# Hybrid decoder layer on one core: v of branch B summed feature block by feature block, all gates of A and B as block-product pairs

## Chip, cores, metric

One core of a Trainium2 chip runs the kernel. The metric is the device time of one execution in microseconds, lower is better. All inputs and outputs lie in HBM and are fp32.

## What is computed

One layer over 1024 prompt tokens and 8 sample tokens, width D = 1024, branches of width 512 (cut from the reference; RMSNorm, LayerNorm and the depthwise convolution are as usual):

```python
mod = jax.nn.silu(c) @ w_ada + b_ada
shift, scale, gate = jnp.split(mod[:, None, :], 3, axis=-1)
h = _rmsnorm(x, norm_g) * (1 + scale) + shift
p = h @ w_in
a_b, a_c, a_h, a_g, b_u, b_v, b_g, c_x, c_g, m_a, m_b, m_c = jnp.split(p, IN_SPLITS, axis=-1)
conv_out, conv_new = _short_conv(a_c * a_h, conv_prev, conv_w, conv_b)
y_a = a_b * conv_out * jax.nn.silu(a_g)
u = jax.nn.gelu(b_u)
v = _layernorm(jax.nn.gelu(b_v), lnv_g, lnv_b)
y_b = _spatial_gate(u, v, sgu_w, sgu_b) * jax.nn.silu(b_g)
...
merged = (jax.nn.sigmoid(m_a) * (y_a @ w_branch[0])
          + jax.nn.sigmoid(m_b) * (y_b @ w_branch[1])
          + jax.nn.sigmoid(m_c) * (y_c @ w_branch[2]))
x = x + gate * (merged @ w_out)
```

`_spatial_gate` mixes v inside blocks of 128 tokens with one lower triangular 128 x 128 matrix per head, adds a bias and multiplies by u.

## The kernel before

**Layout.** Activations lie with the features on the partitions: a tile is 128 features x 1032 tokens. The 1032 columns are two halves of 516 (512 prompt tokens and 4 sample tokens each), so h is eight such tiles, `hhi` and `hlo`. Every fp32 product is three matmuls of rounded parts: high x high, high x low, low x high. A part is made by a copy on ScalarE (high) and a subtraction on VectorE (low), the helper at L86/87.

**Pairs.** Two output tiles of 128 features that share h can be had as one pair (`pair_jobs`, L504 to L567). The contraction is split into two halves of the features and the tokens into their two halves; seven block products of 24 matmuls of 258 columns take the place of eight. For that, sums and differences of token halves of h are needed (`t_sums` L465 to L476, `t_split`, and `t1_split`, which overwrites the first half of hhi and hlo), as are sums of weight blocks, made on VectorE ahead of each pair. A plain tile, not paired, takes 24 x 1032 columns.

**Front and k-loop.** The tokens are cut into three column chunks, `QC`: 416, 360 and 256. The first chunk of x is loaded, squared and summed; from its norm the scale is spread over the partitions (`row_sums` L205, `rsqrt_mean` L212 to L217, `spread` L226, `rstd_all` L241). A conditioning step for each of the eight feature blocks k (`ada_mm` L288, `ada_tr` L296 to L301) gives its scale and shift columns. Then the k-loop runs over the eight feature blocks: h of block k + 1 is built for the first chunk (`h_norm` L247, `h_mod` L254 to L264, `h_lo` L268) while TensorE adds the block k to six output tiles, the four of u and two of the gates of B (`mm3` L357 to L359). The squares of the other chunks are summed on ScalarE and GpSimd inside the loop (`add_square` L195 to L199), and h for them is built at its end; `g1_job` then computes the six tiles for chunks two and three.

**After it.** `bvs_mm` and eight `bv_job` (L697 to L699, 24 matmuls of 512 columns each) give v with tokens on the partitions. Between and behind them run the two other gates of B as plain tiles (`bg_job`), the LayerNorm of v, the sums of token halves (`t_jobs`), four mixing jobs (`sgu_job`, L790 to L805), which multiply u in place (`gate_u` L642), and two plain tiles of A (`ac0`, `ah0`). Then 23 pairs follow, the first of them `ag0`, then `az1`, `ag1` and so on; the merges of the three branches; and the output projection (L1155 to L1157).

**What sets the order.** Each engine runs its instructions in the order in which they are written. A list of `Job`s holds for each: its DMA, its split, its matmuls and its post-work; the planner issues the DMA and the split of a job the stated number of microseconds of matmul time ahead (`ahead`), and puts small post-work (`later`) behind that, as room comes. All loads go by one DMA queue (SP). Matmuls named `warm` (L317) compute nothing that is used; they stand in TensorE's queue among the first row sums.

Of the kernel before, what the change touches and what calls it, by code (L numbers as in the profile page):

```python
# [51 lines left out]
def hybrid_step_kernel(ctx: ExitStack, tc: tile.TileContext, ins, outs):  # L52
# [114 lines left out]
    def load_w1(k):  # L167
        t = S(f"w1r{k}", NG1 * P)
        Q.dma_start(t, ins["w1"][k])
        return t  # L170

    def sum_squares(xk):
        n, nb = QC[0][1:3]
        ps = PS("ss0")
        for k in range(KD):
            sq = S(f"sq0_{k}", n)
            if k == KD - 1:
                V.tensor_tensor(sq, xk[k], xk[k], ALU.mult)
            else:
                A_.activation(sq, xk[k], AF.Square)  # L180
            if k % 2:
                V.tensor_tensor(sq, sq, prev, ALU.add)
                row_sums(ps, sq, n, nb, k == 1, k == KD - 1)
                warm_up(2 if k < 5 else 0)
            prev = sq
        return ps

    def add_square(c, k, xk, acc):

        n = QC[c][1]  # L190
        if k == 0:
            acc[c] = S(f"sqa{c}", n)
        sq = sm.tile([P, 512], F32, tag="sq", name=f"sq{c}_{k}")[:, :n] if k else acc[c]
        if c == 1:
            A_.activation(sq, xk[k], AF.Square)  # L195
        else:
            G_.tensor_tensor(sq, xk[k], xk[k], ALU.mult)
        if k:
            G_.tensor_tensor(acc[c], acc[c], sq, ALU.add)  # L199
# [50 lines left out]
    def h_mod(c, k, th):  # L250
        c0, m, _, at_ = QC[c]
        t, h = th[:, :m], th[:, m:]
        if c == 0:
            V.tensor_scalar(h, t, Ac[:, k, 0:1], Sc[:, k, 0:1], ALU.mult, ALU.add)  # L254
        else:
            for a, b in ((0, at_), (at_ + HS, m)):
                if a < b:
                    A_.activation(h[:, a:b], t[:, a:b], AF.Identity, scale=Ac[:, k, 0:1], bias=Sc[:, k, 0:1])
            s = slice(at_, at_ + HS)
            j = HS * (c - 1)  # L260
            V.tensor_tensor(h[:, s], t[:, s], Ac[:, k, 1 + j : 1 + j + HS], ALU.mult)
            V.tensor_tensor(h[:, s], h[:, s], Sc[:, k, 1 + j : 1 + j + HS], ALU.add)
            V.tensor_copy(hs[:, k, j : j + HS], h[:, s])
        A_.activation(hhi[k][:, c0 : c0 + m], h, AF.Copy)  # L264

    def h_lo(c, k, th):
        c0, m = QC[c][:2]
        V.tensor_tensor(hlo[k][:, c0 : c0 + m], th[:, m:], f32(hhi[k][:, c0 : c0 + m]), ALU.subtract)  # L268

    def build_h(c, ks):  # L270

        th = {}
        n = len(ks)
        for i in range(n + 2):
            if i < n:
                th[i] = h_norm(c, ks[i])
            if 0 <= i - 1 < n:
                h_mod(c, ks[i - 1], th[i - 1])
            if i - 2 >= 0:
                h_lo(c, ks[i - 2], th[i - 2])  # L280
# [1117 lines left out]
```

## Time and profile before

| | |
|---|---|
| device time, median of 3 runs | 953.38 us (951.3 to 953.74) |
| the profiled execution | 952.71 us, of which its span 950.6 us |
| TensorE busy | 915.3 us, 96% |
| VectorE busy | 553.9 us, 58% |
| ScalarE busy | 350.2 us, 37% |
| GpSimd busy | 48.2 us, 5% |
| share of the chain that ended last | TensorE 86%, VectorE 8%, ScalarE 3% |

The span is the time between the first and the last recorded instruction; the rest of the device time lies outside it. A busy time is summed over the whole span, so it averages over stages with different limits. The chain that ended last is followed back from the last instruction: at each step to what released it or to the instruction before it on the same engine. The rows further below are read with these two in mind: a window shows which engine is full in a stretch, a wait shows who was late there, and the time line shows each instruction's start, its duration and, in brackets, the idle time before it with its releaser. A matmul's duration in a row includes the way through the array; the pace is read from the starts.

### The profile page before, as it was taken

The page shows a single profiled execution, that of the slowest core. Times are in us where ns is not written, and L with a number is a line of the kernel's source. Part 1 is how long each engine was busy: PE and PEld are TensorE (multiplying, and loading weights), DVE is VectorE, ACT ScalarE, POOL GpSimd, SP SyncE. Part 2 cuts the span into 40 slices and gives each one's busy share as a digit, 9 for nine tenths or more (in the row PEclk, how much of TensorE's full clock was granted, in tenths as well). Part 3 has the DMA queues.
Part 4 walks back from the last instruction along what each step waited for, and adds up shares of the span by engine and source line. Part 5 has one row for each costly group of instructions (what it writes and reads, how often), then busy time and mean ns, then how long its engine had stood idle before and what let it go on. Part 6 is the DMA issues. An engine that isn't in the chain of part 4 may idle for free.

```text
span 950.6 us, 16189 instructions
## 1 busy us (share of the span) xinstructions
PE 915.3 (96%) x6742; PEld 882.3 (93%) x6742; DVE 553.9 (58%) x1047; ACT 350.2 (37%) x638; POOL 48.2 (5%) x69
## 2 busy tenths in 40 slices
PE   9979999879999999999999999999999999999995
PEld 7759888779999999999999999999999799999995
DVE  4585324698666666665666657644452558673635
ACT  4449525422423334334534534443432310430210
POOL 1250202220000000000000000000000000000001
PEclk7999999989999999999999999999999999999998
DMA  9801400033211122142041330432379826161013
GB/s 336 332 1 46 152 4 23 13 111 131 70 46 68 46 70 85 38 156 90 20 182 45 137 110 1 168 124 100 146 301 376 311 68 222 45 195 30 30 38 112
DMA packets 45466, 108.82 MB, mean 114 GB/s; under 512 B 11465, under 2 KB 18377, under 8 KB 45393
## 3 DMA queue, kind: packets, MB, share of 16 engines
q1 hardware_dynamic: 45392, 107.79, 32.3%
q8 instruction: 53, 0.87, 0.4%
q14 instruction: 21, 0.16, 0.0%
HBM read 83.93 MB, written 23.84 MB: 113 GB/s over the span
## 4 chain that ended last, share of the span: by engine, by line
PE 86%; DVE 8%; ACT 3%; issue 1%; DMA 1%; POOL 0%; SPq 0%; DVEq 0%; ACTq 0%; POOLq 0%
PE o L1155 3%; PE o L1157 3%; PE o L1156 3%; PE g_0B L540 2%; PE g_2B L542 2%; PE g_3B L542 2%; PE g_0B L542 2%; PE g_2B L540 2%; PE g_3B L540 2%; PE g_2B L543 2%; PE g_1B L540 2%; PE g_1B L543 2%; PE g_1B L542 2%; PE g_3B L543 2%; PE g_0B L543 2%; PE bv L697 2%
## 5 line engine op out<-in xcount | busy, mean ns | idle before, releaser
L1155 PE MATMUL o<-mh,woh 128*128 128x388 f32 (+1 forms) x192 | 62.0, 323 | 0.0
L1157 PE MATMUL o<-mh,wol 128*128 128x388 f32 (+1 forms) x192 | 61.4, 320 | 0.0
L1156 PE MATMUL o<-ml,woh 128*128 128x388 f32 (+1 forms) x192 | 61.4, 320 | 0.0
L357 PE MATMUL g<-hhi,w1h 128*128 128x416 f32 (+2 forms) x144 | 48.0, 333 | 2.2 <-ACT hhi L264 2.2
L358 PE MATMUL g<-hlo,w1h 128*128 128x416 f32 (+2 forms) x144 | 46.9, 326 | 1.6 <-DVE hlo L268 1.1
L359 PE MATMUL g<-hhi,w1l 128*128 128x416 f32 (+2 forms) x144 | 46.1, 320 | 0.0
L1155 PEld LDWEIGHTS o<-mh,woh 128*128 128x128 f32 x192 | 36.1, 188 | 0.3
L1156 PEld LDWEIGHTS o<-ml,woh 128*128 128x128 f32 x192 | 36.1, 188 | 0.3
L1157 PEld LDWEIGHTS o<-mh,wol 128*128 128x128 f32 x192 | 36.1, 188 | 0.0
L357 PEld LDWEIGHTS g<-hhi,w1h 128*128 128x128 f32 x144 | 27.2, 189 | 5.1 <-ACT hhi L264 2.8
L358 PEld LDWEIGHTS g<-hlo,w1h 128*128 128x128 f32 x144 | 27.1, 188 | 4.2 <-DVE hlo L268 3.8
L1258 ACT ACTIVATE osq<-xr 128x388 f32<-128x388 f32 (+1 forms) x21 | 10.3, 491 | 48.4 <-DVE xr L1247 28.1
L359 PEld LDWEIGHTS g<-hhi,w1l 128*128 128x128 f32 x144 | 27.1, 188 | 0.1
L86 ACT ACTIVATE mh<-acc 128x516 fp32r<-128x516 f32 (+1 forms) x14 | 9.2, 688 | 44.0 <-DVE acc L1046 44.0
L697 PE MATMUL bv<-bvh,hhi 128*128 128x512 f32 x64 | 25.3, 396 | 0.0
L698 PE MATMUL bv<-bvl,hhi 128*128 128x512 f32 x64 | 25.3, 395 | 0.0
L699 PE MATMUL bv<-bvh,hlo 128*128 128x512 f32 x64 | 25.2, 394 | 0.0
L717 DVE BATCH_NORM_STATS2 bn<-v 128x6 f32<-128x512 f32 x8 | 5.6, 694 | 29.5 <-ACT v L715 29.5
L264 ACT ACTIVATE hhi<-th 128x416 fp32r<-128x416 f32 (+2 forms) x24 | 11.8, 491 | 27.5 <-DVE th L254 26.1
L1252 POOL TENSOR_SCALAR yz<-xr,pk 128x256 f32<-128x256 f32 x2 | 1.9, 929 | 377.1 <-DVE xr L1249 376.7
L1244 DVE SCALAR_TENSOR_TENSOR xr<-o,gt,xr 128x384 f32<-128x384 f32 x16 | 9.8, 613 | 18.7 <-PE o L1157 18.6
L542 PE MATMUL g_3B<-hlo,g_3wB 128*128 128x258 f32 x72 | 20.4, 283 | 0.0
(909 smaller groups left out, 3349.5 us busy)
## 6 DMA issues: line engine op xcount, KB each, us to landing
sig<-sd SPq DMA_DIRECT2D x24, 516.0 KB, 7.0
ada<-in_ada SPq DMA_DIRECT2D x16, 512.0 KB, 7.8
yr<-yd SPq DMA_DIRECT2D x12, 516.0 KB, 9.4
gr<-in_ada_g SPq DMA_DIRECT2D x8, 512.0 KB, 11.3
wor<-in_wo SPq DMA_DIRECT2D x8, 512.0 KB, 6.5
xr<-in_xf SPq DMA_DIRECT2D x8, 512.0 KB, 4.1
sd<-g_0o SPq DMA_DIRECT2D x6, 516.0 KB, 3.8
sd<-g_1o SPq DMA_DIRECT2D x6, 516.0 KB, 2.7
```

The lines of the kernel that those rows point to most:

```text
L357: PE.matmul(o, lhsT=w1hi[k][:, f], rhs=hhi[k][:, cols], start=start, stop=False)
L358: PE.matmul(o, lhsT=w1hi[k][:, f], rhs=hlo[k][:, cols], start=False, stop=False)
L359: PE.matmul(o, lhsT=w1lo[k][:, f], rhs=hhi[k][:, cols], start=False, stop=stop)
L540: PE.matmul(o, lhsT=w[:, 0, f_], rhs=bh, start=start and k == 0, stop=False, skip_group_check=True)
L542: PE.matmul(o, lhsT=w[:, 0, f_], rhs=bl, start=False, stop=False, skip_group_check=True)
L543: PE.matmul(o, lhsT=w[:, 1, f_], rhs=bh, start=False, stop=stop and k == KW - 1, skip_group_check=True)
L697: PE.matmul(ps, lhsT=lh, rhs=whi, start=k == 0, stop=False)
L698: PE.matmul(ps, lhsT=lh, rhs=wlo, start=False, stop=False)
L699: PE.matmul(ps, lhsT=ll, rhs=whi, start=False, stop=k == KD - 1)
L1155: PE.matmul(o, lhsT=wo_h[k][:, w], rhs=cols(mhi[k]), start=start, stop=False)
L1156: PE.matmul(o, lhsT=wo_h[k][:, w], rhs=cols(mlo[k]), start=False, stop=False)
L1157: PE.matmul(o, lhsT=wo_l[k][:, w], rhs=cols(mhi[k]), start=False, stop=stop)
```

## The change

The tokens are no longer cut into three chunks. x is loaded whole, as eight feature tiles of 1032 columns, and its norm is computed for both halves before anything else. The loop over the feature blocks, in the order 0, 4, 1, 5, 2, 6, 3, 7, now builds h of one block for all tokens and adds it to six of the eight token blocks of v, in six PSUM banks (`OUTER`); the two others (`REST`) follow in one job. The sums and differences of token halves are made from x's own tiles inside the loop (`t_steps`; two of them per block pair on GpSimd). u, all gates of B and az0 become pairs; the plain tiles and their helpers are gone. The pairs are now 28, in the order: two gate pairs of the merge (`g1_0`, `g1_1`), two of u, two of gates of B, then az0, ag0 and the rest. The mixing jobs run inside the second pair and leave their result in `mix`; each u and gate pair multiplies into it when it ends (`y_b`). Weights of u and two gates of B are read from the old array by 512-byte rows. The warm-up matmuls before the row sums are 13 and 7 x 6 in a row. The loads of the conditioning weights and of v's weights for the third block are issued twice.

The diff, cut to its core:

```diff
-GC = ((0, 416, 4), (416, 356, 4), (772, 252, 2), (SEQ, NS, 1))
-QC = ((0, 416, 4, None), (416, 360, 4, 96), (776, 256, 2, 252))
+ORDER = (0, 4, 1, 5, 2, 6, 3, 7)
+OUTER = (4, 5, 6, 7, 2, 3)
+REST = (0, 1)
...
+    def load_x(k):
+        xh[k] = S(f"x{k}", T)
+        for hf in range(2):
+            Q.dma_start(xh[k][:, H * hf : H * hf + HP], ins[f"xT{hf}"][:, k, :])
+        G_.tensor_copy(samples(xh[k]), xsm[:, k, :].rearrange("p (h t) -> p h t", h=2))
...
+    def sum_squares():
+        ps = [PS(f"ss{hf}") for hf in range(2)]
+        sq = {}
+        for i, k in enumerate(ORDER):
+            sq[i] = S(f"sq{k}", T)
+            if i < KD - 1:
+                A_.activation(sq[i], xh[k], AF.Square)
+                if i:
+                    V.tensor_tensor(sq[i], sq[i], sq.pop(i - 1), ALU.add)
+                warm_up(6)
+            else:
+                V.tensor_tensor(sq[i][:, H:], xh[k][:, H:], xh[k][:, H:], ALU.mult)
+                A_.activation(sq[i][:, :H], xh[k][:, :H], AF.Square)
+                for hf in (1, 0):
+                    c = cols_of(hf)
+                    V.tensor_tensor(sq[i][:, c], sq[i][:, c], sq[i - 1][:, c], ALU.add)
+                    row_sums(ps[hf], sq[i][:, c], H, NB, True, True)
+        return ps
...
+    def t_steps(k):
+        a, b = xh[k], xh[k + 4]
+        def first():
+            if k % 2 == 0:
+                tt["f", k // 2] = S3(f"t1f{k}", 2, H)
+            G_.tensor_tensor(tt["f", k // 2][:, k % 2, :], a[:, H:], a[:, :H], ALU.subtract)
+            G_.tensor_tensor(b[:, H:], b[:, H:], a[:, H:], ALU.subtract)
+        def hi(n, t):
+            tt[n, k] = S3(f"t{n}_{k}", 2, H, F32R)
+            A_.activation(tt[n, k][:, 0, :], t, AF.Copy)
+        def lo(n, t):
+            V.tensor_tensor(tt[n, k][:, 1, :], t, f32(tt[n, k][:, 0, :]), ALU.subtract)
...
+    def v_mm(i, k, start, stop):
+        c0 = i * P + HS * (i >= NV // 2)
+        w, lh, ll = bv["w", k], hhi[k][:, c0 : c0 + P], hlo[k][:, c0 : c0 + P]
+        PE.matmul(vacc[i], lhsT=lh, rhs=w[:, 0, :], start=start, stop=False)
+        PE.matmul(vacc[i], lhsT=lh, rhs=w[:, 1, :], start=False, stop=False)
+        PE.matmul(vacc[i], lhsT=ll, rhs=w[:, 0, :], start=False, stop=stop)
...
     for i in range(KD):
+        k = ORDER[i]
+        if i + 2 < KD:
+            ada[i + 2] = load_ada(ORDER[i + 2])
+            load_wbv(i + 2)
+        if i % 2:
+            t_todo += t_steps(ORDER[i - 1])
...
+        if i + 1 < KD:
+            n = ORDER[i + 1]
+            ada_tr(n, *sb.pop(i + 1))
+            h_mod(n, 0, 2)
+            w_lo.pop(i + 1)()
+        if i:
+            for j in OUTER[:3]:
+                v_mm(j, k, False, i == KD - 1)
+        if i + 2 < KD:
+            sb[i + 2] = ada_mm(ORDER[i + 2], ada.pop(i + 2))
+            w_lo[i + 2] = split_wbv(i + 2)
+            h_norm(ORDER[i + 2], every)
+        t_next(1 if i + 2 < KD else 2)
+        if i + 1 < KD:
+            h_lo(n, 0, 2)
+        for j in OUTER[3:]:
+            v_mm(j, k, i == 0, i == KD - 1)
+        t_next(1)
...
+    after_h()
+    rest_job()
...
+    mixing = {i + 2: lambda i=i: sgu_job(i) for i in range(KW)}
+    mixing[0] = lambda: Job(mm=lambda: (bvs_sum(), mix_bias()), post=bvs_post, dur=1.5)
+    pairs = [(gates.pop(0), None), (gates.pop(0), mixing)]
+    pairs += [(b_pair("u", (-1 - 2 * i, -2 - 2 * i), i, AF.Gelu_apprx_tanh), None) for i in range(2)]
+    pairs += [(b_pair("bg", ((-5, -6), (0, 1))[i], i, AF.Silu), None) for i in range(2)]
+    for j in range(KW):
+        pairs += [(x, None) for x in a_pairs(j, 2 + 4 * j)]
...
-    for i, (args, after) in enumerate(pairs[1:]):
+    for i, (args, after) in enumerate(pairs):
         pair_jobs(*args, after=after, early_b21=i == 0)
```

Where the change moves instructions, in three places. First TensorE's queue from its start to the second conditioning step. Before (`ss` row sums, `pada` conditioning, `spx` the spread norm):

```order
L317 MATMUL warm<-ones 128x128 x13
L205 MATMUL ss_166<-ones,sq_1_169 104x1 x4
L317 MATMUL warm<-ones 128x128 x2
L205 MATMUL ss_166<-ones,sq_3_181 104x1 x4
L317 MATMUL warm<-ones 128x128 x2
L205 MATMUL ss_166<-ones,sq_5_193 104x1 x4
L205 MATMUL ss_166<-ones,sq_7_202 104x1 x4
L288 MATMUL pada_220<-ada_0_154,sc 32x256 x4
L288 MATMUL pada_220<-ada_1_155,sc 32x256 x4
L226 MATMUL spx_233<-dgx_218,ones 128x416
L296 MATMUL pada_220<-ident,adap_229 128x128 x2
L288 MATMUL pada_250<-ada_0_160,sc 32x256 x4
```

After, in the same stretch:

```order
L279 MATMUL warm<-ones 128x128 x55
L184 MATMUL ss_197<-ones,sq_267 86x1 x6
L184 MATMUL ss_196<-ones,sq_267 86x1 x6
L260 MATMUL pada_308<-ada_0_181,sc 32x256 x4
L260 MATMUL pada_308<-ada_1_182,sc 32x256 x4
L226 MATMUL spx_320<-dgx_293,ones 128x258
L226 MATMUL spx_322<-dgx_293,ones 128x258
L268 MATMUL pada_308<-ident,adap_317 128x128 x2
L226 MATMUL spx_333<-dgx_306,ones 128x258
L226 MATMUL spx_335<-dgx_306,ones 128x258
L260 MATMUL pada_353<-ada_0_186,sc 32x256 x4
L260 MATMUL pada_353<-ada_1_187,sc 32x256 x4
```

All warm-up matmuls now stand ahead of the first row sum, and the row sums of both halves stand together behind them.

Second, VectorE in one feature step of the loop. Before (`adas` the conditioning's sum, `th` the normalised x, `w1l` the weights' low part):

```order
L311 TENSOR_TENSOR w1l_339<-w1r_277,w1h_337 128x768
L298 TENSOR_REDUCE adas_343<-pada_303 128x18
L300 TENSOR_SCALAR Sc<-adas_343,pk 128x9
L301 TENSOR_SCALAR Ac<-adas_343,b_107,pk 128x9
L247 TENSOR_TENSOR th_2_347<-x_2_147,rB_235 128x416
L254 TENSOR_SCALAR th_2_347<-th_2_347,Ac,Sc 128x416
L268 TENSOR_TENSOR hlo_124<-th_2_347,hhi_116 128x416
```

After, a step in which the sums of token halves run too (`x` is now normalised in place, `bvw` is v's weight):

```order
L270 TENSOR_REDUCE adas_489<-pada_449 128x18
L272 TENSOR_SCALAR Sc<-adas_489,pk 128x9
L273 TENSOR_SCALAR Ac<-adas_489,b_107,pk 128x9
L245 TENSOR_TENSOR x_159<-x_159,Ac 128x2x4
L246 TENSOR_TENSOR x_159<-x_159,Sc 128x2x4
L247 COPY hs<-x_159 128x8
L178 TENSOR_TENSOR bvw_460<-bvr_376,bvw_460 128x512
L237 TENSOR_TENSOR x_163<-x_163,rB 128x1032
L299 TENSOR_TENSOR t_0_477<-x_151,t_0_477 128x516
L252 TENSOR_TENSOR hlo_127<-x_159,hhi_119 128x1032
L309 TENSOR_TENSOR x_151<-x_151,x_147 128x516
```

The column-wide operations are now 1032 wide, the sample columns (128x2x4) have operations of their own, and two operations on token halves have come into the step.

Third, ScalarE around the first pair's weights. Before, ahead of `ag0`:

```order
L449 ACTIVATE ac_1975<-ac00p_1885 128x344
L86 ACTIVATE ah0h<-ah0r 128x1024
L86 ACTIVATE t_3_2007<-hb_1962 128x516
L86 ACTIVATE ag0wB_2134<-ag0a 128x512
L86 ACTIVATE ag0wB_2137<-ag0a 128x512
L86 ACTIVATE ag0wT_2143<-ag0s 128x512
```

After, ahead of `g1_0` (`v_857` and `v_858` are the PSUM sums of the two left-over token blocks):

```order
L603 ACTIVATE v_940<-v_857 128x512
L603 ACTIVATE v_940<-v_858 128x512
L91 ACTIVATE g_0wB_947<-g_0a 128x512
L91 ACTIVATE g_0wB_950<-g_0a 128x512
L91 ACTIVATE g_0wT_956<-g_0s 128x512
```

The Gelu of the two left-over blocks of v stands right ahead of the rounding of the first pair's weights, where before a plain tile's evacuation and a block sum stood.

## Rows read from the trace of the kernel before

**Rows 1.** The page, its first part: busy time, share, instructions.

```profile
PE 915.3 (96%) x6742; PEld 882.3 (93%) x6742; DVE 553.9 (58%) x1047; ACT 350.2 (37%) x638; POOL 48.2 (5%) x69
```

**Rows 2.** Windows: stretch, length, busy us by engine, granted clock, DMA share, GB/s.

```profile
0.00:10.00 10.00, 8.89 (x56) 8.61 (x56) 3.18 (x8) 6.76 (x12) 1.96 (x26) 1.00 0.76 239
...
10.00:20.00 10.00, 9.46 (x56) 5.59 (x56) 4.77 (x14) 3.45 (x7) 0.71 (x3) 0.51 1.03 417
...
50.00:60.00 10.00, 7.05 (x35) 5.52 (x34) 8.81 (x17) 1.81 (x4) 9.53 (x12) 1.00 0.01 2
...
190.00:200.00 10.00, 5.38 (x25) 5.31 (x25) 9.79 (x16) 1.27 (x2) 1.50 (x1) 0.66 0.20 63
```

**Rows 3.** Windows of TensorE alone, one microsecond after its longest wait.

```profile
193.00:194.00 1.00, 0.00 (x0) 0.50 0.00 0
```

**Rows 4.** TensorE's waits: us in total, times, longest.

```profile
PE ac00p L430 <- DVE mixb L798: 4.6, 1, 4.6
```

**Rows 5.** Time line, first matmul of three feature steps: start, busy us, engine, line.

```profile
35.15 0.44 PE L357 MATMUL g<-hhi,w1h 128*128 128x416 f32 x1
...
39.99 0.44 PE L357 MATMUL g<-hhi,w1h 128*128 128x416 f32 x1
...
53.03 0.43 PE L357 MATMUL g<-hhi,w1h 128*128 128x416 f32 x1
```

**Rows 6.** Time line of TensorE, where its next kinds of work begin.

```profile
111.00 1.92 PE L763 MATMUL bvs<-bvr,hs 128*32 128x512 f32 x16
...
112.85 0.50 PE L697 MATMUL bv<-bvh,hhi 128*128 128x512 f32 x1
...
157.54 0.63 PE L430 MATMUL bg20p<-hhi,bg2h 128*128 128x344 f32 x3
...
182.78 1.97 PE L790 MATMUL mix<-ws,v 128*64 128x128 f32 x32
...
224.23 0.28 PE L540 MATMUL ag0B<-hhi,ag0wB 128*128 128x258 f32 x1
...
248.64 0.28 PE L540 MATMUL az1B<-hhi,az1wB 128*128 128x258 f32 x1
...
268.76 0.28 PE L540 MATMUL ag1B<-hhi,ag1wB 128*128 128x258 f32 x1
```

**Rows 7.** The chain that ended last, its piece on x: start, us, what.

```profile
2.67 6.63 DMA x<-in_xT
```

**Rows 8.** Time line of TensorE in the front: warm-up, sums, first h matmul.

```profile
1.10 5.88 PE L317 MATMUL warm<-ones 128*128 128x128 f32 x26 [1.10 <-DVE ones L107]
...
9.02 0.69 PE L317 MATMUL warm<-ones 128*128 128x128 f32 x4
...
10.72 1.55 PE L205 MATMUL ss<-ones,sq 128*104 128x1 f32 x8 [0.36 <-DVE sq L182]
...
20.43 0.45 PE L357 MATMUL g<-hhi,w1h 128*128 128x416 f32 x1
```

**Rows 9.** Time line, one feature step: conditioning on TensorE, reduce and norm on VectorE.

```profile
41.86 1.07 PE L288 MATMUL pada<-ada,sc 128*32 128x256 f32 x16
...
42.56 0.22 DVE L298 TENSOR_REDUCE adas<-pada 128x18 f32<-128x72 f32 x1
...
43.16 0.58 DVE L247 TENSOR_TENSOR th<-x,rB 128x416 f32<-128x416 f32 x1
```

**Rows 10.** Groups by line and shape: count, busy us, mean ns, idle before.

```profile
L642 DVE TENSOR_TENSOR u<-u,sgb 128x1032 f32<-128x1032 f32 x4 | 4.8, 1228 | 0.1
...
L715 ACT ACTIVATE v<-bv 128x512 f32<-128x512 f32 x8 | 4.8, 599 | 31.2 <-PE bv L699 31.2
```

**Rows 11.** Time line: one VectorE operation alone, and beside GpSimd.

```profile
194.67 0.69 DVE L802 TENSOR_TENSOR u<-u,mixb 128x512 f32<-128x512 f32 x1
...
198.50 2.42 POOL L465 TENSOR_TENSOR ha<-hhi,hlo 128x1032 f32<-128x1032 f32 x1 [13.70 <-DVE t L87]
...
199.06 2.42 DVE L802 TENSOR_TENSOR u<-u,mixb 128x512 f32<-128x512 f32 x1
```

More of the change, by code (lines that the diff above doesn't have):

```diff
@@ L165, in load_ada, with load_wbv, split_wbv @@
         return t
[L167 to L199, printed above, removed]
+    bv = {}
+    NV = SEQ // P
+    def load_wbv(i):
+        k = ORDER[i]
+        if i % 2 == 0:
+            bv["pair"] = S3(f"bvr{i}", 2, W)
+        bv["raw", k] = bv["pair"][:, i % 2, :]
+        Q.dma_start(bv["raw", k], ins["wbv"][:, k, :])
+    def split_wbv(i):
+        k = ORDER[i]
+        w = bv["w", k] = S3(f"bvw{k}", 2, W, F32R)
+        A_.activation(w[:, 0, :], bv["raw", k], AF.Copy)
+        return lambda: V.tensor_tensor(w[:, 1, :], bv["raw", k], f32(w[:, 0, :]), ALU.subtract)
     def row_sums(ps, sq, n, nb, start, stop):
@@ L250, in h_mod @@
[L250 to L280, printed above, removed]
+    rs_ = {"B": S("rB", T)}
+    def rstd_all(hf, dg):
+        ps = [spread(f"x{hf}{s}", dg[:, s * HC : (s + 1) * HC], HC, NB // 2) for s in range(2)]
+        for s in range(2):
+            A_.activation(rs_["B"][:, H * hf + HC * s : H * hf + HC * s + HC], ps[s], AF.Copy)
@@ new lines, in t1_split @@
+    def t1_split():
+        for k in range(KW):
+            split(tt["f", k // 2][:, k % 2, :], hhi[k][:, H:], hlo[k][:, H:])
+        del tt["f", 0], tt["f", 1]
+    vacc = {}
+    def v_mm(i, k, start, stop):
[4 more added lines that the diff above has]
+        PE.matmul(vacc[i], lhsT=ll, rhs=w[:, 0, :], start=False, stop=stop)
@@ new lines, in hybrid_step_kernel @@
+    warm_up(13)
+    Q.dma_start(xsm, ins["xT2"])
+    for k in ORDER:
+        load_x(k)
+    ada = {}
+    for i in range(3):
+        load_wbv(i)
+        ada[i] = load_ada(ORDER[i])
+    every = slice(0, T)
+    ss = sum_squares()
+    dg = {1: rsqrt_mean("x1", ss[1], H, NB)}
+    w_lo = {0: split_wbv(0)}
+    dg[0] = rsqrt_mean("x0", ss[0], H, NB)
+    sb = {0: ada_mm(ORDER[0], ada.pop(0))}
+    w_lo.pop(0)()
+    rstd_all(1, dg[1])
+    h_norm(ORDER[0], cols_of(1))
+    ada_tr(ORDER[0], *sb.pop(0))
@@ L385, in hybrid_step_kernel @@
+    del rs_["B"], bv["pair"]
+    dg = ss = None
+    t_next(2)
     jobs = []
@@ L714, in v_stat, with v_keep, rest_job @@
-    def v_stat(i, v, ps, n):
-        A_.activation(v, ps, AF.Gelu_apprx_tanh)
+    def v_keep(i):
+        if ("v", i // 2) not in bv:
+            bv["v", i // 2] = S3(f"v{i // 2}", 2, W)
+        v = bv["v", i // 2][:, i % 2, :]
+        A_.activation(v, vacc.pop(i), AF.Gelu_apprx_tanh)
+        later(0.8, lambda: v_stat(i, v, P))
+    def rest_job():
+        def mm():
+            for i in REST:
+                vacc[i] = PS(f"v{i}")
+            for k in ORDER:
+                for i in REST:
+                    v_mm(i, k, k == ORDER[0], k == ORDER[-1])
+                del bv["w", k]
+        def post():
+            for i in REST:
+                v_keep(i)
+            later(0.6, v_scale)
+            for j in range(NV):
+                later(1.3, lambda j=j: v_norm_t(j))
+        Job(small_dma, None, mm, post, dur=11.2)
@@ new lines, in post, with b_pair @@
+            if g == KW - 1:
+                later(0.5, small_copy)
+                for x in [x for x in bv if x not in ("col", "w00")]:
+                    del bv[x]
+        Job(None, None, mm, post, dur=1.9)
+    def b_pair(name, n, i, func):
+        def post(o0, o1, ps):
+            for c in range(2):
+                A_.activation(o1[:, c * HC : (c + 1) * HC], ps[c], func)
+            A_.activation(o1[:, H:], o1[:, H:], func)
+            A_.activation(o0, o0, func)
+            for j, o in enumerate((o0, o1)):
+                later(1.3, lambda o=o, g=2 * i + j: y_b(g, o))
+        return f"{name}{i}", n[0], n[1], post
```

375 lines of the change are left out of this document (102 added, 273 removed).

## Prediction

> **What bounds the kernel now.** I read the page's busy times first, then the windows, the waits of TensorE, and last the time line of TensorE around the places that the change touches. TensorE is busy in 96% of the span [rows 1], so the time is nearly its matmuls plus its few stalls, and a change pays by taking matmuls or stalls out of TensorE's queue. The windows show where the stalls are: 50 to 60 us, where TensorE is busy 7.05 of 10 while VectorE (8.81) and GpSimd (9.53) are full, and 190 to 200, where it is busy 5.38 with VectorE at 9.79 [rows 2]. The largest single wait is 4.6 us, ac0 waiting for VectorE's mixed bias [rows 4]; at its end the granted clock is 0.50, the 1.2 GHz level [rows 3].
>
> From 248.64 us on, where the pair az1 starts, the stretches are even: the next pair starts at 268.76, so a pair costs 20.12 us [rows 6]. From there 22 pairs, the merges and the output projection follow, 950.6 - 248.64 = 702.0 us. In the changed kernel 22 pairs, the same merges and the same projection are left when az0 starts. So I work out when **az0 starts after** and compare it with 248.64.
>
> **Columns first.** Ten feature tiles (u 4, gates of B 4, ac0, ah0) of 24 x 1032 columns go, 247,680 columns; five more pairs come, each 7 x 24 x 258 = 43,344 columns, 216,720 in all. v of B costs the same 192 matmuls of 512 columns. 30,960 columns less, at the pair's own pace of 20.12 us / 43,344 = 0.464 ns, is 14.4 us. The rest of the answer is in what the new front and the first pairs wait for.
>
> **The front, to the first v matmul.** All of x must land before a norm is known: 4.2 MB instead of 1.7. The first 10 us moved 239 GB/s, so 2.4 MB, the next ten 417 GB/s [rows 2], which puts x at 10 + 1.8 MB / 417 GB/s = 14.4 us; before, its x had landed at 2.67 + 6.63 = 9.3 us [rows 7] and the first matmul on h started at 20.43, 11.1 us later [rows 8]. The same chain (last square, sum, row sums, reciprocal root, diagonal, spread, norm, modulation, rounding) stands in the changed kernel, on 516 columns instead of 416 and with a second half beside it: 25.5 us plus a little. A second claim is the 55 warm-up matmuls ahead of the row sums in TensorE's queue. The first 26 passes took 5.88 us, later four took 0.69 [rows 8]; 55 matmuls are 110 passes, so they end by 1.1 + 5.9 + 84 x 0.17 = 21.5 us at most, and from the row sums to the first h matmul it took 20.43 - 10.72 = 9.7 us [rows 8]: 31.2 us as the upper end. I take **28.0**, the middle of 25.5 and 31.2.
>
> **The eight feature steps.** A step on TensorE is 18 matmuls of 512 columns, 16 passes of the conditioning and two transposes. 192 such matmuls took 157.54 - 112.85 us [rows 6], 0.2328 each, so 4.19 us, the conditioning 1.07 and the time from there to the next matmul counted in, with 0.4 for the transposes: 5.65 us. (The Trainium skill, "TensorE: Matmul & The Clock Gate", section "Wait — 56ns, not 53.3ns?", gives 215.7 ns for a warm 512-column matmul start to start; this trace has 232.8, and the measurement decides. By the page the 192 v matmuls would cost 3.3 us less in all, an estimate.)
>
> VectorE's step: from the reduce to the next big operation 43.16 - 42.56 = 0.60 [rows 9], three small ones on the sample columns (taken as 0.2 each, the reduce's row being 0.22), the weight's low part 0.69 (a 512-wide operation, [rows 11]), normalising and h's low part on 1032 columns 1.23 each [rows 10]: 4.35. The sums of token blocks, now in the loop, add about 12 operations of 0.69 over the steps, 1.0 a step: 5.35, still under TensorE's 5.65. Then GpSimd. A 512-wide VectorE operation took 0.69 us alone and 2.42 beside a GpSimd operation of 2.42 us [rows 11]. Six of the new GpSimd operations fall into the loop, of 516 columns each; half of 2.42 for half the columns is 1.2 us, 7.3 us in all or 0.9 a step, if VectorE loses every one in full: 6.25. (The Trainium skill, "SBUF — State Buffer", section "SBUF: two separate sides", says that GpSimd and VectorE share a pair of ports as an exclusive lock that whoever starts first keeps for the whole instruction, for a VectorE operation with two SBUF inputs. It speaks against putting sums on GpSimd here. The trace agrees where GpSimd began first; by the rule VectorE loses between nothing and the 7.3 us.) I take **6.0** a step, 48.0 for eight. Lower end 5.65, TensorE alone. Upper end from the old loop: its step was 39.99 - 35.15 = 4.84 us free and (53.03 - 39.99) / 2 = 6.52 where GpSimd worked beside it [rows 5], 1.35 times; 5.35 x 1.35 = 7.2.
>
> **From the loop to az0.** The samples' v, 1.85 us (111.00 to 112.85, [rows 6]). The two token blocks left over, 48 x 0.2328 = 11.2. Behind them ScalarE's order matters: the two Gelu of these blocks stand ahead of the rounding of the first pair's weights, so TensorE has nothing while two Gelu and one rounding of 0.60 us [rows 10] and a 0.69 subtraction pass: **2.5** (0 if the wait falls elsewhere, 4 with two more such operations between). Six pairs (two gates, u, gates of B), 6 x 20.12 = 120.7. Five small jobs (samples and bias counted as one like a mixing job of 1.97, [rows 6]): 10.2 with the transposes. Last, stalls of the first pairs: ag0, the first pair of before, took 248.64 - 224.23 = 24.4 us [rows 6], 4.3 over a pair's pace, while VectorE caught up; now the first two pairs run beside eight normalisations, the left-over block sums and the mixing. One such stall at least is likely, three are the worst: I take **6.5**, bounds 0 and 13.
>
> Sum: 28.0 + 48.0 + 1.85 + 11.2 + 2.5 + 120.7 + 10.2 + 6.5 = **229.0 us** against 248.64, 19.7 less. What hides the moved work: u times its gate and the mixing stood in VectorE's full stretch from 190 to 200 us [rows 2, 11]; now mix is kept and multiplied when each pair ends, beside pairs of 20.12 us, in which VectorE has room by the even starts in [rows 6]. The weights of two conditioning blocks and of v are fetched twice, 1.25 MB, 3 us of transfer at 417 GB/s; it is cover for nothing only if the front is bound by DMA, which the 28.0 already allows.
>
> The profiled execution took 952.71 us, its span 950.6, so 2.1 lie outside; it is 0.7 under the median 953.38. 950.6 - 19.7 + 2.1 = **933.0**.
>
> **Rivals.**
> (a) VectorE and GpSimd block each other through the loop, a step is 7.2 us: 48.0 becomes 57.6, time 942.6. For it speaks [rows 5]; against, that GpSimd was busy 9.53 of 10 us there [rows 2] and now would be some 7 of 48.
> (b) All covers hold: front 26, steps 5.65, no wait for Gelu, stalls 2: 26 + 45.2 + 1.85 + 11.2 + 120.7 + 10.2 + 2 = 217.2, time 921.2.
> (c) Every doubtful term at its upper end: 31.2 + 57.6 + 1.85 + 11.2 + 4 + 120.7 + 10.2 + 13 = 249.8, time 953.8: the columns are saved and all given back to waits. It needs four misses at once.
> (d) Slower: TensorE falls to the 1.2 GHz level in the step loop because it waits for VectorE in every step. A 512-column matmul then takes 0.466, a step 2 x 5.65 = 11.3 us, 5.3 more than 6.0. The gain of 19.7 is gone once four of the eight steps run so; with seven the time is 933 + 37 = 970. For it: after a wait of 4.6 us the clock was 0.50 [rows 3, 4], and 0.51 over 10 to 20 us, where the front's small matmuls run [rows 2]. Against: from 50 to 60 us TensorE was idle 30% in pieces and the clock stayed 1.00 [rows 2]; the loop's expected idle share is 6%.
> (e) The kernel does not do what it says: the order of the queues shows both the missing tiles and five more pairs, so this has no chance of its own.
>
> **Chances.** Forecast (927 to 939) 0.62; (a) 0.15; (b) 0.14; (c) 0.04; (d) 0.05. A measurement of this kernel tells 0.3%, 2.9 us, from no change. Faster is forecast, (a) and (b): 0.91; same 0.04; slower 0.05. The range takes in (a) and (b) with their bounds, 921 to 946, and leaves (c), (d) and some tails out.
>
> **What would show it.** Right: az0 starts near 229 us; the first v matmul (the first 512-column one) at 28; steps of about 6 us at clock 1.00; one wait of 2 to 3 us after the left-over blocks, released by ScalarE or VectorE; pairs g0 and g1 longer than 20.12 by some 6 us together, and all later pairs at 20.1. Wrong if: the first v matmul comes after 31; VectorE is full in the loop and steps are 7 us; the granted clock in the loop is 0.5; the pairs from az0 on are not at 20.1, which would break the assumption that all behind stays as it was.

## The result, and the profile after

The changed kernel takes **929.5 us** (median, 927.4 to 931.31) against 953.55 for the kernel before: ratio 0.9752, 95% interval 0.9726 to 0.9778. Measured again beside two of the experiments it took 930.67 us, ratio 0.9772 (0.9755 to 0.979). Forecast were 933.0 with a range of 921 to 946, and faster. The profiled execution took 927.4 us with a span of 925.7.

The page's first part, as [rows 1]:

```profile
PE 903.6 (98%) x6910; PEld 873.2 (94%) x6910; DVE 570.6 (62%) x1041; ACT 354.5 (38%) x638; POOL 21.1 (2%) x49
```

TensorE is busy 98% of the span instead of 96, and 11.7 us less in all. Where that fell shows in windows cut at the places that the sum named: to the first v (before: first h) matmul, through the loop, to the first pair of the even stretch, and the rest. Columns: stretch, length, busy us of TensorE, its weight loads, VectorE, ScalarE, GpSimd (instructions), granted clock, DMA share, GB/s. Before:

```profile
0.00:20.43 20.43, 18.79 (x112) 14.64 (x113) 8.38 (x23) 10.21 (x19) 2.68 (x28) 0.75 0.90 330
20.43:111.00 90.57, 82.87 (x561) 72.35 (x560) 53.78 (x145) 54.03 (x100) 19.97 (x24) 1.00 0.37 134
111.00:248.64 137.64, 125.75 (x816) 111.93 (x815) 83.10 (x144) 46.91 (x76) 21.41 (x9) 0.98 0.19 62
248.64:950.60 701.96, 687.94 (x5260) 683.36 (x5258) 408.64 (x737) 239.08 (x444) 4.14 (x8) 0.99 0.33 116
```

After:

```profile
0.00:29.43 29.43, 25.56 (x177) 21.47 (x177) 16.67 (x38) 15.58 (x24) 2.56 (x32) 0.85 0.92 343
29.43:77.12 47.69, 44.97 (x257) 30.31 (x255) 45.78 (x80) 28.68 (x40) 13.30 (x8) 0.98 0.34 133
77.12:224.36 147.24, 145.81 (x1223) 139.06 (x1223) 92.21 (x174) 72.92 (x136) 1.09 (x1) 1.00 0.29 91
224.36:925.70 701.34, 687.23 (x5260) 682.34 (x5258) 415.99 (x751) 237.31 (x440) 4.13 (x8) 0.99 0.33 115
```

The last stretch is the same, 701.96 and 701.34 us. All of the gain lies ahead of it: 248.64 became 224.36, 24.3 us less. TensorE's idle time there fell from 21.2 us (20.43 - 18.79, 90.57 - 82.87, 137.64 - 125.75) to 8.0, so 13.2 us came from waits. Its busy time fell by 11.1 us. That is 3.3 less than the 14.4 us of columns; the front's own busy time grew by 6.8 us (25.56 against 18.79), warm-ups and a low clock among it, which these windows don't separate. So the fewer waits gave about as much (13.2 us) as the fewer matmuls (11.1 us net), where the sum had 14.4 of 19.7 from columns.

The time line of TensorE at the points of the sum, the counterpart of [rows 6, 8] (start, busy us, engine, line, operation; in brackets the idle time before it and its releaser):

```profile
19.33 2.23 PE L184 MATMUL ss<-ones,sq 128*86 128x1 f32 x24 [2.77 <-DVE sq L204]
...
21.48 1.93 PE L260 MATMUL pada<-ada,sc 128*32 128x256 f32 x16
...
29.43 0.79 PE L330 MATMUL v<-bvw,hhi 128*128 128x512 f32 x1
...
77.12 1.92 PE L684 MATMUL bvs<-bvr,hs 128*32 128x512 f32 x16
...
78.97 0.50 PE L330 MATMUL v<-bvw,hhi 128*128 128x512 f32 x1
...
91.59 0.39 PE L516 MATMUL g_0B<-hhi,g_0wB 128*128 128x258 f32 x1 [1.20 <-ACT g_0wB L91]
...
112.57 0.28 PE L516 MATMUL g_1B<-hhi,g_1wB 128*128 128x258 f32 x1
...
143.88 0.28 PE L516 MATMUL u0B<-hhi,u0wB 128*128 128x258 f32 x1
...
224.36 0.28 PE L516 MATMUL az0B<-hhi,az0wB 128*128 128x258 f32 x1
```

And TensorE's waits (total, times, longest), of which 4.6 us for the mixed bias stood in [rows 4]:

```profile
PE ss L184 <- DVE sq L204: 2.8, 1, 2.8
...
PE v L332 <- DVE hlo L252: 2.1, 3, 1.3
...
PE g_0B L516 <- ACT g_0wB L91: 1.2, 1, 1.2
...
PE g_0B L519 <- DVE g_0wB L92: 0.2, 1, 0.2
```

That wait is gone: the mixing jobs now run inside the second pair.

### The profile page after: what moved, and what is told of

The parts are those of the page before. It is cut to its first block, busy times and chain, and to the rows that moved or that the text cites. A ratio compares the mean times of both kernels' runs of the same rounds, so it can differ in the third digit from the quotient of the medians.

```text
span 925.7 us, 16539 instructions
## 1 busy us (share of the span) xinstructions
PE 903.6 (98%) x6910; PEld 873.2 (94%) x6910; DVE 570.6 (62%) x1041; ACT 354.5 (38%) x638; POOL 21.1 (2%) x49
## 4 chain that ended last, share of the span: by engine, by line
PE 90%; DVE 5%; ACT 1%; issue 1%; DMA 1%; SPq 0%; DVEq 0%; ACTq 0%
PE o L1063 3%; PE o L1065 3%; PE o L1064 3%; PE g_1B L516 2%; PE g_0B L519 2%; PE g_0B L516 2%; PE g_2B L516 2%; PE g_2B L518 2%; PE g_3B L519 2%; PE g_2B L519 2%; PE g_3B L516 2%; PE g_1B L519 2%; PE g_3B L518 2%; PE g_1B L518 2%; PE g_0B L518 2%
## 5 line engine op out<-in xcount | busy, mean ns | idle before, releaser
L332 PE MATMUL v<-bvw,hlo 128*128 128x512 f32 x64 | 26.1, 408 | 2.2 <-DVE hlo L252 2.1
L330 PE MATMUL v<-bvw,hhi 128*128 128x512 f32 x64 | 27.0, 422 | 0.0
L331 PE MATMUL v<-bvw,hhi 128*128 128x512 f32 x64 | 25.5, 398 | 0.0
L516 PE MATMUL g_0B<-hhi,g_0wB 128*128 128x258 f32 x72 | 20.5, 284 | 1.2 <-ACT g_0wB L91 1.2
L519 PE MATMUL g_0B<-hhi,g_0wB 128*128 128x258 f32 x72 | 20.4, 284 | 0.2 <-DVE g_0wB L92 0.2
L516 PE MATMUL g_1B<-t,g_1w 128*128 128x258 f32 x72 | 20.5, 285 | 0.0
L516 PE MATMUL g_1B<-hhi,g_1wB 128*128 128x258 f32 x72 | 20.5, 285 | 0.0
L516 PE MATMUL g_0B<-t,g_0w 128*128 128x258 f32 x72 | 20.5, 284 | 0.0
L516 PE MATMUL g_2B<-t,g_2w 128*128 128x258 f32 x72 | 20.4, 284 | 0.0
L519 PE MATMUL g_1B<-hhi,g_1wB 128*128 128x258 f32 x72 | 20.4, 283 | 0.0
L518 PE MATMUL g_0B<-hlo,g_0wB 128*128 128x258 f32 x72 | 20.4, 283 | 0.0
L519 PE MATMUL g_3B<-hhi,g_3wB 128*128 128x258 f32 x72 | 20.4, 283 | 0.0
L519 PE MATMUL g_2B<-hhi,g_2wB 128*128 128x258 f32 x72 | 20.4, 283 | 0.0
## 6 DMA issues: line engine op xcount, KB each, us to landing
gr<-in_ada_g SPq DMA_DIRECT2D x8, 512.0 KB, 10.2
```

The lines of the kernel that those rows point to most:

```text
L330: PE.matmul(vacc[i], lhsT=lh, rhs=w[:, 0, :], start=start, stop=False)
L331: PE.matmul(vacc[i], lhsT=lh, rhs=w[:, 1, :], start=False, stop=False)
L332: PE.matmul(vacc[i], lhsT=ll, rhs=w[:, 0, :], start=False, stop=stop)
L516: PE.matmul(o, lhsT=w[:, 0, f_], rhs=bh, start=start and k == 0, stop=False, skip_group_check=True)
L518: PE.matmul(o, lhsT=w[:, 0, f_], rhs=bl, start=False, stop=False, skip_group_check=True)
L519: PE.matmul(o, lhsT=w[:, 1, f_], rhs=bh, start=False, stop=stop and k == KW - 1, skip_group_check=True)
```

## The experiments

All but `b_az0` are edits of the changed kernel. Starts of az0 are read from each trace as above; between two profiles of the changed kernel they moved by about a microsecond (224.4 and 225.5). The difference lies in the front, in TensorE's clock. In the second profile the row sums began earlier, but at the low level, 0.50, and took 3.65 us instead of 2.23:

```profile
19.03 3.65 PE L184 MATMUL ss<-ones,sq 128*86 128x1 f32 x24 [3.75 <-DVE sq L204]
```

The first v matmul came at 30.55 there instead of 29.43. The loop behind it was the same, 47.7 us. So a loop is compared by its own length below, from the first v matmul to the samples' v, and not by when it ends.

**1. GpSimd's sums on VectorE (`t_dve`).**

```diff
-            G_.tensor_tensor(tt["f", k // 2][:, k % 2, :], a[:, H:], a[:, :H], ALU.subtract)
-            G_.tensor_tensor(b[:, H:], b[:, H:], a[:, H:], ALU.subtract)
+            V.tensor_tensor(tt["f", k // 2][:, k % 2, :], a[:, H:], a[:, :H], ALU.subtract)
+            V.tensor_tensor(b[:, H:], b[:, H:], a[:, H:], ALU.subtract)
```

> The changed kernel with the eight GpSimd operations of the token-half sums (two per pair of feature blocks) moved to VectorE. Theory (GpSimd locks VectorE out): in the changed kernel's trace the nine-column scale operation took 1.0 to 1.4 us instead of 0.23 where it met a GpSimd operation of 1.3 to 1.7 us, about 1 us lost for each of six operations in the loop; on VectorE each costs 0.61 to 0.69, so the loop (29.4 to 77.1 us, 47.7) gets shorter by 6 x (1.0 - 0.65), about 2 us, and az0 starts at 222 instead of 224.4. Rival (GpSimd's work is hidden, the loop is bound elsewhere): VectorE gets 6 x 0.65 = 4 us more work and the loop becomes 51 to 52 us long, az0 at 228.

Measured 927.64 us, ratio 0.9723 (0.9703 to 0.9743). The loop's window, columns as above:

```profile
30.63:74.80 44.17, 43.85 (x262) 30.73 (x262) 41.95 (x86) 28.86 (x40) 0.00 (x0) 0.98 0.35 132
```

44.17 us instead of 47.69, TensorE busy in 43.85 of it. The theory holds, and more strongly than it said: VectorE got eight operations more and the loop lost 3.5 us. The other runs bear it out: in all seven profiles in which the loop is as changed (both of the changed kernel, `split_first`, `more_warm`, `no_warm`, `one_load` and `pe_sums`) it took 47.69 to 47.74 us, whether it began at 27.4 or at 38.8 us, and in the three with the sums on VectorE (`t_dve`, `best`, `best_w29`) 43.7 to 44.1. The whole time shows little of it, 927.64 against 929.5 us, and the intervals of the two ratios overlap. az0 came at 223.8, only 0.5 earlier, because the first v matmul was at 30.6 in this run, where the clock fell before the row sums, and the first two pairs took 1.8 us more, at a granted clock of 0.54 to 0.61 from 90 to 94 us. In the changed kernel's own trace the price is seen directly, a time line of VectorE and GpSimd:

```profile
37.54 1.30 POOL L292 TENSOR_TENSOR x<-x,x 128x516 f32<-128x516 f32 x1 [6.03 <-DVE hlo L252]
...
37.73 1.14 DVE L272 TENSOR_SCALAR Sc<-adas,pk 128x9 f32<-128x9 f32 x1
...
40.41 2.17 POOL L291 TENSOR_TENSOR t1f<-x 128x516 f32<-128x516 f32 x1 [1.58 <-ACT x L244]
...
41.47 2.21 DVE L252 TENSOR_TENSOR hlo<-x,hhi 128x1032 fp32r<-128x1032 f32 x1
...
44.46 0.23 DVE L272 TENSOR_SCALAR Sc<-adas,pk 128x9 f32<-128x9 f32 x1
```

The nine-column operation takes 0.23 us when free and 1.14 where GpSimd had begun 0.19 us before it; it ends when GpSimd's does. h's low part on 1032 columns takes 2.21 instead of 1.23 behind a GpSimd operation. That the one holds the other is read from these overlaps; the runs show the price of having the operations on GpSimd.

**2. The sums of token halves behind the loop (`t_after`).**

```diff
-        t_next(1 if i + 2 < KD else 2)
...
-        t_next(1)
...
-    t_next(2)
```

> The changed kernel with the sums of token halves (GpSimd's and VectorE's) taken out of the feature loop and done behind it, beside the left-over blocks and the first pair. Theory (VectorE sets the loop's pace; the first pairs wait little because VectorE is only half busy there): the loop is TensorE's own, 44 to 45 us instead of 47.7, and the 20 operations of VectorE (13 us) with eight of GpSimd (10 to 13 us) behind it are not done when the first pair needs them: the wait between the left-over blocks and the end of the second pair grows from 1.9 to 8 us or more, az0 at 228 to 232. Rival (the loop is TensorE's already, VectorE hidden): loop 47.7, az0 at 231 to 235. Rival (the stall in the first pairs doesn't hang on VectorE's room): loop 44 to 45 and az0 at 221.

Measured 935.92 us, one run. The loop's window, and TensorE's waits at the first pair:

```profile
30.63:77.80 47.17, 44.68 (x254) 30.50 (x254) 35.27 (x66) 27.51 (x36) 12.54 (x8) 0.98 0.32 124
```

```profile
PE g_0B L513 <- ACT g_0wB L91: 3.8, 1, 3.8
PE g_0B L516 <- DVE g_0wB L92: 3.7, 1, 3.7
```

The edit takes out the calls that put the sums between the steps; a call that the kernel already has, ahead of the left-over blocks, then issues them all. VectorE's operations left the loop (35.27 us busy instead of 45.78) but GpSimd's, which have a queue of their own, stayed in it (12.54 us), so the edit did half of what was meant. The loop was 47.17 us, half a microsecond shorter. So the theory that VectorE's load sets the loop's pace fell. The loop's and az0's times (47.2 and 233.5) are near those of the first rival, but its reason, that TensorE itself needs 47.7, fell with experiment 1, where TensorE did the loop in 44.2. Together with experiment 1: it is the GpSimd operations that lengthen it, by holding single VectorE operations that stand between conditioning and h. In this run four of them ran in a row from 47.32 to 53.32 us, and VectorE's small operations of 9, 9 and 8 columns beside them read

```profile
49.93 0.92 DVE L272 TENSOR_SCALAR Sc<-adas,pk 128x9 f32<-128x9 f32 x1
50.76 1.33 DVE L273 TENSOR_SCALAR Ac<-adas,b,pk 128x9 f32<-128x9 f32 x1
52.12 1.22 DVE L245 TENSOR_TENSOR x<-x,Ac 128x8 f32<-128x8 f32 x1
```

From h's low part in this step to the next (47.17 to 55.41) it was 8.2 us; the steps without GpSimd took 4.3 to 5.7. The second half came as expected: the waits around the first pair grew by 6.1 us, the samples' v to u0 took 153.1 - 77.8 = 75.3 us instead of 66.8, and az0 came at 233.5, past the 228 to 232.

**3. One pair in place of two plain tiles, in the kernel before (`b_az0`).**

```diff
-        if g % 2:
-            win_job(*plain.pop(0), ahead=(18.0, 12.0))
...
-    for i, (args, after) in enumerate(pairs[1:]):
+    for i, (args, after) in enumerate(pairs):
```

> One part of the change alone, in the kernel before: the two plain tiles of A (ac0, ah0) leave and az0 becomes a pair ahead of ag0, so 24 pairs. Theory (columns at the pair's pace): 2 x 24,768 - 43,344 = 6,192 columns fewer, at 0.464 ns 2.9 us faster, and the waits of 4.6 and 1.1 us at the two plain tiles stay or move: about 950.7 against 953.6. Rival (the plain tiles were the cover of the mixing jobs): the mixing jobs stand in a row, TensorE waits for VectorE's mixing and multiplying before the first pair, and the time is the same or up to 8 us longer.

Measured 958.6 us, ratio 1.0066 (1.005 to 1.0082): slower by about 6, though 2.9 us of columns are saved. The window of the pair az0, and its waits:

```profile
199.60:235.90 36.30, 28.28 (x169) 27.20 (x170) 29.89 (x50) 10.24 (x21) 1.40 (x1) 0.78 0.28 102
```

```profile
PE az0B L540 <- DVE mixb L798: 4.4, 2, 3.4
...
PE az0B L543 <- DVE az0wB L87: 2.5, 1, 2.5
```

A pair of 20.12 us takes 36.3. VectorE is busy 29.89 us of them with token sums, mixing, multiplying and the pair's own weight sums, and at a clock of 0.78 the matmuls that run are slower too: TensorE's busy time is 28.28 us, so of the 16.2 us over a pair's pace half are waits and half are slower matmuls. The rival was right. **Here a pair did not pay: TensorE waited for VectorE's mixing and for the pair's weight sums.** The change made room on VectorE by taking the token sums into the loop and the mixing into a later pair. What share of the loss belongs to the pair's own weight sums and what to the mixing jobs, which stand in a row without plain tiles between them, this run does not separate.

**4. The first pair's weights ahead of the Gelu (`split_first`).**

```diff
-                ahead=(24.0, 6.0))
+                ahead=(24.0, 12.0 if early_b21 and i == 0 else 6.0))
```

> The changed kernel with the first weight block of the first pair rounded before the left-over token blocks of v end, so ahead of their two Gelu on ScalarE. Theory (the wait of 1.2 + 0.23 us at 90.2 to 91.6 us comes from ScalarE's order): the first pair starts within 0.3 us of the end of the left-over blocks, 11.2 us after they begin, and az0 comes 1.4 us earlier relative to the samples' v. Rival (the next block's weights, still behind the Gelu, are late in its place): the wait moves into the pair and az0 stays.

Measured 929.06 us, one run. The pair starts without a wait, and a new one stands inside it:

```profile
PE g_0B L516 <- ACT g_0u L528: 1.6, 1, 1.6
```

az0 came 146.9 us after the samples' v instead of 147.2. The rival was right: ScalarE's queue is late at this place whichever piece goes first.

**5. The clock in the front: ten more warm-ups (`more_warm`), 42 fewer (`no_warm`), and the third block loaded once (`one_load`).**

```diff
-    warm_up(13)
+    warm_up(23)
```

```diff
-                warm_up(6)
```

```diff
-    for i in range(3):
+    for i in range(2):
         load_wbv(i)
```

> The changed kernel with ten more warm-up matmuls at the start, so that TensorE has work until the row sums can start (the warm-ups end at 16.55, the row sums begin at 19.33 and the granted clock is 0.50 from 21 to 31 us). Theory A (the idle 2.8 us bring the clock down): the clock stays 1.00 over 20 to 30 us, conditioning passes take 1.07 instead of 1.93 and the first v matmul comes 2 to 3 us earlier, at 27. Theory B (the small matmuls of row sums, conditioning and spread don't hold the clock, as in the kernel before, where it fell at 10.4 us without a long pause): clock 0.50 again, first v matmul at 29.4 within 0.5.

> The changed kernel without the 7 x 6 warm-up matmuls (13 stay). They end at 16.55 us, before VectorE has the squares. Theory (what counts is whether TensorE is at work right up to the row sums): without them the clock is 0.50 when the row sums begin, 24 passes take 3.6 us instead of 2.2 as in the run where it had fallen, first v matmul at 30.8 instead of 29.4, az0 at 225.8. Rival (the warm-ups buy nothing, since the clock is 0.50 over 21 to 31 us anyway): first v matmul at 29.4 within 0.4.

> The changed kernel with the weights of the third feature block (1.25 MB) loaded once instead of twice. Theory (the loop is bound by VectorE, not by transfers): az0 starts within 0.5 us of 224.4. Rival (the front is bound by DMA until 40 us, share 1.03 there): the later conditioning weights come 3 us earlier, the conditioning of the fourth block starts at 36 to 37 instead of 39.35 and az0 at 221.5 to 223.

Measured 926.87, 930.42 and 929.11 us, one run each. The changed kernel's own times spread over 4 us, so these three are compared by their traces. TensorE in the window from 20 to 30 us (length, busy, clock, DMA share, GB/s), changed kernel first, then with ten more:

```profile
20.00:30.00 10.00, 10.00 (x60) 0.54 1.03 414
```

```profile
20.00:30.00 10.00, 7.90 (x65) 1.00 1.03 413
```

With ten more, the wait ahead of the row sums was 0.5 instead of 2.8 us, the clock stayed at the 2.4 GHz level, and the first v matmul came at 27.4 instead of 29.4, az0 at 222.4: theory A's numbers. From the row sums' start to the first v matmul it was 8.4 us (19.00 to 27.42) instead of 10.1 (19.33 to 29.43), so by these two profiles the low clock costs about 1.7 us. The loop was 47.69 us in both, so it costs nothing behind the front. Without the 42, TensorE waited 12.2 us, the clock was 0.50, and the first v matmul came at 30.8, az0 at 225.8, both as expected. One load instead of two left az0 at 224.8 and the loop at 47.7: the second load is hidden, though the DMA share is 1.03 there.

**6. Squares summed on TensorE (`pe_sums`).**

```diff
-                if i:
-                    V.tensor_tensor(sq[i], sq[i], sq.pop(i - 1), ALU.add)
-                warm_up(6)
...
+            if i % 2 and i < last:
+                V.tensor_tensor(sq[i], sq[i], sq.pop(i - 1), ALU.add)
+                for hf in (1, 0):
+                    row_sums(ps[hf], sq[i][:, cols_of(hf)], H, NB, i == 1, False)
+                warm_up(2)
```

> The changed kernel with x's squares summed on TensorE (row sums of each pair of blocks, as the kernel before did) instead of by a chain of seven 1032-wide additions on VectorE; the 7 x 6 warm-up matmuls become 3 x 2. Theory (the front waits for VectorE's chain: the last x tile is there at 16.5, VectorE begins its square at 17.76 and TensorE's row sums at 19.33): the norm's first instruction moves from 20.4 to about 18.8, the first v matmul from 29.4 to about 28, az0 to about 223. Rival (the front is bound by the conditioning weights behind x in the DMA queue, or by the low clock): first v matmul stays at 29 or later, az0 at 224 to 225.

Measured 938.41 us, ratio 0.9841 (0.9826 to 0.9856), 9 us worse. TensorE's row sums:

```profile
11.09 3.67 PE L184 MATMUL ss<-ones,sq 128*86 128x1 f32 x24 [5.26 <-DVE sq L201]
...
15.62 3.58 PE L184 MATMUL ss<-ones,sq 128*86 128x1 f32 x24
...
20.06 3.58 PE L184 MATMUL ss<-ones,sq 128*86 128x1 f32 x24
...
24.50 7.10 PE L184 MATMUL ss<-ones,sq 128*86 128x1 f32 x48
```

After a wait of 5.26 us the clock was 0.50 and 24 passes took 3.6 us, against 2.23 in the changed kernel and 1.97 in `more_warm`, where the clock stayed at 1.00; five such sets make 18 us on TensorE, which became the front's bound: first v matmul at 38.8, az0 at 233.7. Neither expectation held. That VectorE's chain ends the front is not refuted, but this edit put something longer in its place.

**7. The edits together (`best`, `best_w29`).** Edits 1, 4 and 5 (one load), with 12 and with 16 more warm-ups.

> The changed kernel with four edits: GpSimd's sums on VectorE, 12 more warm-up matmuls, the third block loaded once, the first pair's first weights rounded before the Gelu. Theory (the pieces add): first v matmul at 27.4, loop 44.2 us as in the run with the sums on VectorE, left-over blocks to the first pair without a wait, az0 at about 219.5 against 224.4, time 924.5 to 925. Rival (what is saved in the loop comes back in the first pair, where the run with the sums on VectorE lost 1.8 us at a granted clock of 0.5 to 0.6): az0 at 221 to 222, time 926.5.

> The run with four edits, now with 16 instead of 12 more warm-up matmuls. In the run with 12 TensorE still waited 0.80 us before the row sums and the granted clock fell at 22.7 us; in the run with 10 alone it waited 0.47 and the clock stayed at 1.00. Theory (the wait before the row sums decides): no wait, clock 1.00 to 30 us, first v matmul at 27.4 instead of 28.35, az0 at 218.8. Rival (the fall has to do with the small matmuls themselves, and which run shows it is chance): the clock falls between 21 and 24 us again, first v matmul at 28.3 or, with the row sums pushed back, later.

Measured 924.89 us, ratio 0.9718 (0.970 to 0.9735), and 925.2 us, ratio 0.9714 (0.970 to 0.9729), the latter beside the changed kernel's 930.67 on the same chip: 5 us faster than the changed kernel. The loops took 43.7 and 44.1 us, az0 came at 219.7 and 221.3. With 12, az0 and the time came as the theory had them (219.5 and 924.5 to 925), the first v matmul 0.95 us later than it said and the loop 0.5 shorter. In both runs the first pair, whose first weights are now early, waits 2.3 us inside, and the first two pairs take 1.8 us more than in the changed kernel, as in `t_dve`. The clock, however, fell at 22 to 23 us with 12 and at 21 with 16, although TensorE waited only 0.8 and 0.9 us before the row sums; the run with 16, from 20 to 30 us:

```profile
20.00:30.00 10.00, 10.00 (x62) 0.55 1.03 410
```

The rival's numbers came: with four more warm-ups the first v matmul was at 29.5, no earlier. So why it held in `more_warm` and not here is open: the wait before the row sums differed by 0.3 us, and each is one profile.

## Why the prediction was right, point by point

| step | forecast | measured |
|---|---|---|
| first v matmul | 28.0 | 29.4 |
| eight steps | 48.0 | 47.7 |
| samples' v | 1.85 | 1.85 |
| left-over blocks | 11.2 | 11.25 |
| wait behind them | 2.5 | 1.4 |
| six pairs, five small jobs, stalls of the first pairs | 120.7 + 10.2 + 6.5 | 132.8 |
| az0 starts | 229.0 | 224.4 |
| from there to the end | 702.0 | 701.3 |

- **The front** was 1.4 us longer. The 28.0 was a choice between two bounds, and the middle of 25.5 and 31.2 is 28.35. The low clock was not what the sum lacked: its durations came from a front that ran at 0.51 as well. In the kernel before, conditioning and spread read

```profile
12.20 1.93 PE L288 MATMUL pada<-ada,sc 128*32 128x256 f32 x16
14.30 1.76 PE L226 MATMUL spx<-dgx,ones 104*128 104x416 f32 x2 [0.18 <-DVE dgx L217]
16.42 1.93 PE L288 MATMUL pada<-ada,sc 128*32 128x256 f32 x16
```

In the changed kernel conditioning takes 1.93 and 1.94, spread 2.09 and 1.93. From the row sums that end VectorE's chain to the first matmul on h it is 10.1 us, where [rows 8] had 9.7. What the lower bound had too short is the time to the row sums: 25.5 less 9.7 is 15.8, and they came at 19.33. The warm-ups did not hold them up, as the upper bound had it: they ended at 16.55. VectorE's additions of 1032 columns did, one behind the other, and then the last block's halves:

```profile
11.26 6.59 DVE L197 TENSOR_TENSOR sq<-sq,sq 128x1032 f32<-128x1032 f32 x5 [0.45 <-ACT sq L195]
...
17.76 0.69 DVE L200 TENSOR_TENSOR sq<-x 128x516 f32<-128x516 f32 x1
...
18.49 1.30 DVE L204 TENSOR_TENSOR sq<-sq,sq 128x516 f32<-128x516 f32 x2
```

That the measured front lies between bounds that erred both ways is in part luck.

- **The steps** came out within 0.3 us for all eight, and for the reason given: 5.65 of TensorE and a loss to GpSimd. `t_dve` sizes the two: 5.52 and 0.44 a step, where 5.65 and 0.35 had been taken. The loss was counted otherwise, though: six operations of 1.2 us, 7.3 in all, of which a part was taken; there were eight, GpSimd's queue running ahead, with 13.30 us in all, and 3.5 of them were lost. VectorE's full tenths in the loop are partly blocked time; taking 10.5 us of its busy time out gained 0.5. The Trainium skill ("SBUF — State Buffer", section "SBUF: two separate sides") names two SBUF inputs, or a 2-port mode, as the condition for the lock. Here also the nine-column operation, with one tile and a per-partition scalar, was held for 1.14 us; whether it ran in such a mode no run shows.
- **The pace** of the 512-column matmuls was again 0.2328 us and not the 0.2157 that the Trainium skill gives ("TensorE: Matmul & The Clock Gate", section "Wait — 56ns, not 53.3ns?"), so the left-over blocks took what [rows 6] said.
- **The wait behind the left-over blocks** was there, released by ScalarE as forecast, at 1.4 us instead of 2.5: the first of the two Gelu began at 89.72 us, before the last matmul of the blocks had ended.
- **The stalls of the first pairs** were the term that was mis-sized: 0.9 us, all in the first pair, instead of 6.5. Of these 0.2 are a wait. The second pair with the five small jobs took 31.3 us, 1.0 more than their 20.1 and 10.2, but TensorE was busy in all of it, so the small jobs were 11.2 us and no stall. The price of 6.5 was worked out from ag0's 4.3 us, and that belonged to a place where VectorE had more to do. The windows, ag0 before:

```profile
224.23:248.64 24.41, 20.66 (x171) 20.24 (x169) 19.57 (x37) 8.10 (x18) 0.00 (x0) 1.00 0.24 82
```

The first two pairs after, then the second alone:

```profile
91.59:143.90 52.31, 52.08 (x487) 49.23 (x488) 36.27 (x79) 27.26 (x47) 0.00 (x0) 1.00 0.23 73
...
112.57:143.88 31.31, 31.31 (x320) 28.83 (x319) 22.39 (x48) 13.95 (x24) 0.00 (x0) 1.00 0.36 111
```

VectorE is busy 80% of ag0's window and 69% of the first two pairs', the token sums being done by then. `t_after` and `b_az0` show the other side: with the sums behind the loop the waits are back, and in the old place a pair loses 16 us. The busy share alone gives no price: in `b_az0` it was 82%, near ag0's, and the loss four times as large. The account of the gain has the same fault: beside the 14.4 us of columns the net was 9.9 us, not 5.3.
- **The rivals.** (b) was nearer on the stalls (2 us) and wrong on the front; (a) fell with the loop's 47.7. (c) and (d) did not occur, though (d)'s mechanism did at a small price: the clock was at 0.50 from 21 to 31 us, after TensorE's wait of 2.8 us for VectorE, and cost about 1.7 us, all of it ahead of the loop. (The window of [rows 3], on which (d) leaned, lies inside that kernel's wait of 4.6 us, which ended at 194.69; the clock was 0.50 there until 198.)
- **The rest** of the span was unchanged, so the assumption that 22 pairs and all behind them stay was right within 0.7 us. The total came within 3.5 us because the front was longer while the stalls were shorter, and because the profiled execution, the fastest of four, was 2.1 under the median: by the trace alone az0 was 4.6 early.

## What to carry to other kernels

A stall seen on one instruction belongs to the place, not to the instruction: price the stalls of moved work by what the helping engine still has to do at the new place, and check that by its busy time and by the waits there. A transform that saves matmuls but asks VectorE for more, like the pairs here, first needs VectorE's other work moved to where TensorE has its own. GpSimd is no free helper beside a chain of VectorE operations: eight small sums there cost this loop 3.5 us more than the same sums on VectorE itself.

## What had not been expected of the hardware

A nine-column VectorE operation of 0.23 us ends when the GpSimd operation ends that began just before it, and takes 1.0 to 1.4 us. Twenty-four row-sum passes of one column take 2.0 us at the 2.4 GHz level (`more_warm`) and 3.6 at the 1.2 GHz level (`pe_sums`), so a norm summed on TensorE depends on the clock that precedes it.
